# A scan's triangular solve beside the next step's key products, its state kept in PSUM

## The chip, the cores and the metric

The kernel runs on one core of a Trainium2 chip. The metric is the device time of one execution in microseconds (us), the median of three runs. PE is the matmul engine (PEld its weight loads), DVE the vector engine, ACT the scalar engine, POOL the general one, SP the engine that issues the DMAs.

## What is computed

Two layers of a bidirectional encoder run on two groups of 512 tokens, 1024 wide, in 32-bit floats. Layer 0 is RWKV-7 time mixing; its core is a scan per head (16 heads of 64), once forward and once backward in time, and the two results are summed:

```python
def _wkv7_scan(r, decay, k, v, a, b, reverse):
    def step(s, inp):
        r_t, w_t, k_t, v_t, a_t, b_t = inp
        sa = jnp.einsum('bhvk,bhk->bhv', s, a_t)
        s = s * w_t[:, :, None, :] + sa[..., None] * b_t[:, :, None, :] + v_t[..., None] * k_t[:, :, None, :]
        return s, jnp.einsum('bhvk,bhk->bhv', s, r_t)
    ...
    _, y = lax.scan(step, s0, xs, reverse=reverse)
```

Around it stand projections (`xn @ w_r`, `w_k`, `w_v`, `w_z`, an output product with `w_o`), low-rank decays and rates, norms and a SiLU gate. Layer 1 is a neighbourhood attention over an 8 x 64 grid with its own projections. Each layer is normed before and after and added to its input.

## The kernel before

Tokens lie along the free axis, 128 channels (two heads) on the partitions. The scan is done by chunks: 512 tokens are 8 chunks of 64 (`NCH`, `L`). A *pair block* is four heads, `(s, pb)`: group `s` of two, block `pb` of four, so eight of them (`self.todo`), and each takes 8 steps, one chunk of the forward scan and one of the backward scan in each step: 64 steps in all (`self.steps`).

One step (`step`, with `near` and `outer`) does on PE, always with heads on the two halves of the partitions:

- STATE, line 1111: 16 products of the carried state `S` with the chunk's factors, into PSUM tile `zy`; not in a block's first step.
- AKV, line 1117: 8 products with the masked key products `AK`, added to the same tile. ACT scales the sum to `Z` (line 1123).
- SOLVE, line 1133: 8 products of `Z` with the inverse `MT` of the chunk's triangular matrix, into the first half of a bank `us`. ACT copies the two directions into `X` (line 1144); the other half of `X` holds the values, from DMA.
- IDENT, line 1138: in steps 1 to 6 of a block, two products with an identity matrix put the old state into the other half of the bank `us`.
- near, line 1041: 8 key products of the *next* step, into a spare part of `zy`; DVE masks them to `AK` (line 1045).
- SO, line 1149: 8 products over 128 rows add the chunk's own part to the state in `us`; DVE multiplies by the decay and writes the next `S` (line 1159).
- Y, line 1154: 8 products over 128 rows make the outputs; ACT (chunks 0 to 3) or DVE (4 to 7) takes them to `y`.
- OUTER, line 1066: 16 products of 128 columns whose masked results `R` (DVE) and `Tm` (ACT) the step's Y and SO read.

SOLVE and near use 64 x 64 quarters of the array on its diagonal: rows 0 to 63 with columns 0 to 63, and rows 64 to 127 with columns 64 to 127.

While the scan runs, other work fills PE: the *products* (lines 758 to 760, three 128 x 512 matmuls for each of 8 k in a column of weights; 608 such triples) for the projections, `lora` (807, 808) and `grams` (934) for the next block's factors, transposes, and `inverse` (948 on), which inverts the triangular matrices: 30 rounds of two DVE instructions (964, 965), transposes on DVE, then two small sets of products (993, 995). The inverses run one block after another, at a low rank, during the steps of the block before.

The order on PE, DVE and ACT is fixed when the program is built. `weave` takes threads (one each for steps, near, outer, factors, inverse, products and so on) piece by piece; a class `Clock` adds up costs, a piece is taken when its inputs are ready by that clock, and among the ready ones PE pieces come last and the rank decides. A `yield "P"` ends a piece, so that another thread's piece may come between; a change of tile size on PE costs 100 in `Clock.matmul` only where it waits for running tiles.

After the scan the rest (`rest`: the last columns, attention, output products) runs in the scheduler's own order.

Of the kernel before, what the change touches and what calls it, by code (L numbers as in the profile page):

```python
# [18 lines left out]
P = 128  # L19
# [30 lines left out]
class Clock:  # L50
# [132 lines left out]
    def matmul(self, i, ins, n, t):  # L183
# [10 lines left out]
        if self.mode != ts and self.tiles:  # L194
            t = max([t] + [x + 100.0 for x in self.tiles.values()])
            self.tiles = {}
        self.mode = ts
# [36 lines left out]
class Trunk:  # L234
# [782 lines left out]
    def fetch_x(self, st):  # L1017
# [4 lines left out]
        for d in range(2):  # L1022
            self.load(
                st.X[half(1 - e[d]), d].rearrange("t h g c -> t h (g c)"),
                sp["vt", s][pb, i % 2, i // 2, :, :, d].rearrange("h t g c -> t h (g c)"))

    def near(self, q):

        nc, st = self.nc, self.steps[q]
        half = lambda h: slice(64 * h, 64 * h + 64)  # L1030
# [3 lines left out]
            lambda c: max(c.at([st.ab.tensor.name]), 0.0 if q else room(c)))  # L1034
        ab, e = st.ab, st.e
        st.AK = self.t("AK", (P, 2, 2, L), self.NAK, F32, self.front)
        ak = self.steps[q - 1].room if q else self.p("pm", (P, 2, 2, L))
        for g in range(2):
            for dd in range(2):
                for h in range(2):  # L1040
                    nc.tensor.matmul(
                        ak[half(h), dd, g], ab[half(h), dd, g, 1 + e[dd]], ab[half(h), dd, g, 2 - e[dd]], start=not q, stop=True,
                        skip_group_check=True)
        yield "D"
        nc.vector.tensor_tensor(st.AK, ak, self.mstrict.unsqueeze(1).unsqueeze(1).broadcast_to([P, 2, 2, L]), op=ALU.mult)
        self.did["AK"] += 1

    def outer(self, q):
# [9 lines left out]
        for d in range(2):  # L1058
            for g in range(2):
                for a in range(2):  # L1060
                    for h in range(2):
# [5 lines left out]
                            f[half(a), h, 0, d, g] if st.last else f[half(a), h, :, d, g], ab[half(h), d, g, 2 * e[d] + a],  # L1067
# [17 lines left out]
    def step(self, q):  # L1085
# [18 lines left out]
        st.room = zy[:, 0, 256:512].rearrange("p (d g t) -> p d g t", d=2, g=2)  # L1104
# [20 lines left out]
        yield "P", lambda: did["inverse"] > st.n and free2(), lambda c: max(c.at(name(Z, self.formed[key][1])), room2(c))  # L1125
# [3 lines left out]
        for g in range(2):  # L1129
# [703 lines left out]
```

## Time and profile before

| | us |
|---|---|
| median of three runs | 1713.48 (1712.95 to 1714.0) |
| the profiled execution's own time | 1717.21 |
| its span, first to last instruction | 1715.1 |
| PE busy | 1601.5 (93%) |
| DVE busy | 1207.0 (70%) |
| ACT busy | 965.4 (56%) |

The steps run from about 285 to 1067 us of the span. Per-instruction times of small matmuls overlap (each record holds its pipeline's end), so what a bunch of them takes is read from the distance between the starts of one bunch and the next.

### The profile page before, as it was taken

What the parts mean: (1) busy time and instruction counts of PE and PEld (TensorE: products, weight loads), DVE (VectorE), ACT (ScalarE), POOL (GpSimd) and SP (SyncE); (2) the same over time, 40 slices, a digit from 0 to 9 for tenths busy, and PEclk for the clock granted to TensorE, in tenths of its full rate; (3) what the DMA queues carried; (4) which work ended last, traced back from release to release, by engine and by line L of the source; (5) the groups of instructions that cost most, each with busy time, mean ns of one, the idle gap of its engine ahead of it and who ended that gap; (6) DMA issues with size and microseconds to landing.
All of it is one profiled execution on the core that took longest, in us unless ns stands there. A gap on an engine that the chain in (4) does not pass through costs nothing.

```text
span 1715.1 us, 46051 instructions
## 1 busy us (share of the span) xinstructions
PE 1601.5 (93%) x18816; PEld 1229.3 (72%) x18816; DVE 1207.0 (70%) x2645; ACT 965.4 (56%) x1950; POOL 20.7 (1%) x64
## 2 busy tenths in 40 slices
PE   7999879998989999999998878999999999999998
PEld 6766657675756676777776767787777787777776
DVE  8986789695978888898879756423556586555574
ACT  5444766665666485667664533334556665555462
POOL 0000000000000000000000000000000000000000
PEclk9989979898999999999998999999999999999999
DMA  5436778675665677878755756744564247555553
GB/s 205 166 117 208 245 268 262 197 252 188 216 213 187 202 237 228 257 229 252 238 188 175 253 178 201 245 148 153 167 202 135 94 148 270 166 160 166 161 166 99
DMA packets 240820, 336.26 MB, mean 196 GB/s; under 512 B 53696, under 2 KB 119360, under 8 KB 240608
## 3 DMA queue, kind: packets, MB, share of 16 engines
q1 hardware_dynamic: 240608, 333.31, 60.6%
q8 instruction: 148, 2.42, 0.6%
q14 instruction: 64, 0.52, 0.1%
HBM read 227.71 MB, written 105.51 MB: 194 GB/s over the span
## 4 chain that ended last, share of the span: by engine, by line
PE 50%; DVE 8%; ACT 4%; DMA 4%; issue 2%; SPq 0%; DVEq 0%; ACTq 0%
PE pg L424 6%; PE pg L425 5%; PE pg L426 5%; PE pm L758 5%; PE pm L759 4%; PE pm L760 4%; PE pm L1367 3%; PE po L1395 2%; PE pt L1382 2%; PE pf L1066 1%; DMA cab<-dab 1%; PE us L1133 1%; DVE ab L839 1%; PE us L1149 1%; DVE etmp L964 1%
## 5 line engine op out<-in xcount | busy, mean ns | idle before, releaser
L758 PE MATMUL pm<-act,whi 128*128 128x512 f32 x608 | 265.5, 437 | 11.5 <-ACT act L741 7.7
L759 PE MATMUL pm<-act,whi 128*128 128x512 f32 x608 | 245.8, 404 | 8.5 <-DVE act L743 6.9
L760 PE MATMUL pm<-act,wlo 128*128 128x512 f32 x608 | 244.3, 402 | 0.0
L424 PE MATMUL pg<-act,whi 128*128 128x512 f32 x448 | 181.5, 407 | 0.0
L425 PE MATMUL pg<-act,whi 128*128 128x512 f32 x448 | 178.4, 398 | 0.0
L426 PE MATMUL pg<-act,wlo 128*128 128x512 f32 x448 | 177.9, 397 | 0.0
L374 DVE TENSOR_TENSOR wlo<-raw,whi 128x512 fp32r<-128x512 f32 x156 | 107.1, 688 | 91.9 <-ACT whi L373 79.5
L373 ACT CAST whi<-raw 128x512 fp32r<-128x512 f32 x156 | 96.4, 618 | 131.6 <-PE pg L425 62.5
L721 DVE TENSOR_TENSOR wlo<-raw,whi 128x512 fp32r<-128x512 f32 x152 | 103.6, 685 | 82.5 <-ACT whi L719 82.0
L758 PEld LDWEIGHTS pm<-act,whi 128*128 128x128 f32 x608 | 117.7, 194 | 48.8 <-ACT act L741 9.6
L759 PEld LDWEIGHTS pm<-act,whi 128*128 128x128 f32 x608 | 118.2, 194 | 33.3 <-DVE act L743 9.7
L719 ACT CAST whi<-raw 128x512 fp32r<-128x512 f32 x152 | 93.3, 621 | 81.5 <-PE pm L759 69.9
L760 PEld LDWEIGHTS pm<-act,wlo 128*128 128x128 f32 x608 | 118.2, 194 | 26.2
L424 PEld LDWEIGHTS pg<-act,whi 128*128 128x128 f32 x448 | 84.3, 188 | 23.8 <-issue 9.1
L425 PEld LDWEIGHTS pg<-act,whi 128*128 128x128 f32 x448 | 84.3, 188 | 18.4 <-issue 3.5
L426 PEld LDWEIGHTS pg<-act,wlo 128*128 128x128 f32 x448 | 84.2, 188 | 18.2 <-issue 2.2
L965 DVE TENSOR_TENSOR N<-etmp,N 128x30 f32<-128x30 f32 (+14 forms) x240 | 79.8, 332 | 8.3
L1378 ACT ACTIVATE sb<-sb,mx 128x256 f32<-128x256 f32 x128 | 64.1, 502 | 37.7 <-DVE mx L1377 37.2
L1375 DVE CUSTOM_DVE_ANT_0 sb<-pm,bias 128x256 f32<-128x256 f32 x128 | 50.3, 421 | 44.9 <-PE pm L1367 34.1
L964 DVE TENSOR_TENSOR etmp<-N 128x30 f32<-128x30 f32 (+14 forms) x240 | 78.2, 326 | 3.5
L1066 PE MATMUL pf<-cab 64*64 64x128 f32 (+1 forms) x2048 | 69.4, 271 | 8.0 <-DMA cab<-dab 4.5
L1081 ACT COPY Tm<-pf 128x512 f32<-128x512 f32 x56 | 32.8, 587 | 78.0 <-DVE R L1074 78.0
(366 smaller groups left out, 3361.8 us busy)
## 6 DMA issues: line engine op xcount, KB each, us to landing
dab<-ab SPq DMA_DIRECT2D x32, 1024.0 KB
cab<-dab SPq DMA_DIRECT2D x64, 512.0 KB
raw<-in_w_in_dram SPq DMA_DIRECT2D x128, 256.0 KB
bias<-in_rpb_dram SPq DMA_DIRECT2D x32, 384.0 KB
raw<-in_w_z_dram SPq DMA_DIRECT2D x32, 256.0 KB
dz<-tmp SPq DMA_DIRECT2D x32, 256.0 KB
raw<-in_w_k_dram SPq DMA_DIRECT2D x32, 256.0 KB
dk<-tmp SPq DMA_DIRECT2D x32, 256.0 KB
```

Of the source, the lines that this page charges most:

```text
L373: self.nc.scalar.copy(hi, src)
L374: (eng or self.nc.vector).tensor_tensor(lo, src, hi.bitcast(F32), op=ALU.subtract)
L424: nc.tensor.matmul(ps, hi, x[k][0], start=(k == 0), stop=False)
L425: nc.tensor.matmul(ps, hi, x[k][1], start=False, stop=False)
L426: nc.tensor.matmul(ps, lo, x[k][0], start=False, stop=(k == KT - 1))
L719: nc.scalar.copy(hi, raw[h])
L721: nc.vector.tensor_tensor(lo, raw.pop(h), hi.bitcast(F32), op=ALU.subtract)
L758: nc.tensor.matmul(ps, hi[:, at], xh, start=(k == 0), stop=False)
L759: nc.tensor.matmul(ps, hi[:, at], xl, start=False, stop=False)
L760: nc.tensor.matmul(ps, lo[:, at], xh, start=False, stop=(k == KT - 1))
L964: vt.tensor_tensor(tv, N[:, q + 1:, q:q + 1].broadcast_to([P, n, q]), N[:, q:q + 1, :q].broadcast_to([P, n, q]), op=ALU.mult)
L1066: end = nc.tensor.matmul(f[half(a), h, 0, d, g] if st.last else f[half(a), h, :, d, g], ab[half(h), d, g, 2 * e[d] + a], rt if st.last els ...
```

## The change

SOLVE now multiplies half `a` of the rows into half `1 - a` of the columns, the quarters off the diagonal, so `X` keeps its solved part in the other half, its values are loaded into the half that is left, and OUTER writes its rows the other way round. SOLVE's result lies in `zy`, in the spare part that near's results had, and near's results in the same part of the tile's second bank. Where the next chunk's factors are in by the planner's clock when a step's SOLVE is taken, near's 8 products are issued between SOLVE's, two after every other one (`keys_by_step`); else near is a bunch of its own as before.

The bank `us` is now one tile for all steps of a block. SO adds to what stands there, and after DVE has made `S`, ACT copies `S` back into it, in steps 0 to 5 (`act.copy(so, st.S)`); IDENT is gone. There is no `yield` between SO and Y. The planner's clock adds 100 for a change to whole-array matmuls and 50 for other changes of tile size, so that the order changes in many places.

```diff
@@ Clock.matmul
             self.tiles = {}
+            c += 100.0 if ts == (128, 128) else 50.0
@@ fetch_x
-                st.X[half(1 - e[d]), d].rearrange("t h g c -> t h (g c)"),
+                st.X[half(e[d]), d].rearrange("t h g c -> t h (g c)"),
@@ near, its products now in a generator
+    def keys_by_step(self, q, ak):
...
+        for g in range(2):
+            for d in range(2):
+                for h in (1, 0):
+                    nc.tensor.matmul(
+                        ak[half(h), d, g], ab[half(h), d, g, 1 + e[d]], ab[half(h), d, g, 2 - e[d]], start=not q, stop=True,
+                        skip_group_check=True)
+                    yield
@@ outer
-                            f[half(a), h, 0, d, g] if st.last else f[half(a), h, :, d, g], ab[half(h), d, g, 2 * e[d] + a],
+                            f[half(1 - a), h, 0, d, g] if st.last else f[half(1 - a), h, :, d, g], ab[half(h), d, g, 2 * e[d] + a],
@@ step
-        st.room = zy[:, 0, 256:512].rearrange("p (d g t) -> p d g t", d=2, g=2)
+        u = zy[:, 0, 256:512].rearrange("p (h g v) -> p h g v", h=2, g=2)
+        st.room = zy[:, 1, 256:512].rearrange("p (d g t) -> p d g t", d=2, g=2)
...
-        us = self.p("us", (P, 2, 4, HD))
-        u = us[:, 0].rearrange("p (h g) v -> p h g v", h=2)
-        for g in range(2):
-            for h in range(2):
-                for d in range(2):
-                    r = half(e[d])
-                    nc.tensor.matmul(u[r, h, g], mt[r, h, st.i, g], Z[r, h, g], start=True, stop=True)
-        so = us[:, 1].rearrange("p (d g) v -> p d g v", d=2)
-        if st.i and not st.last:
-            for h in range(2):
-                nc.tensor.matmul(
-                    us[half(h), 1].rearrange("p a v -> p (a v)"), self.ident[half(h), 64 * h:64 * h + 64],
-                    before.S[half(h)].rearrange("p d g v -> p (d g v)"), start=True, stop=False, skip_group_check=True)
+        if st.i == 0:
+            self.so = self.p("us", (P, 2, 2, HD))
+        so = self.so
...
+        merged = after and did["fetch"] > q + 1 and self.clock.at([after.ab.tensor.name]) <= self.clock.pe() + self.EPS
+        if merged:
+            k = self.keys_by_step(q + 1, st.room)
+        for g, h in gh:
+            for a in range(2):
+                if a:
+                    next(k, None)
+                    next(k, None)
+                nc.tensor.matmul(
+                    u[half(1 - a), h, g], mt[half(a), h, st.i, g], Z[half(a), h, g], start=False, stop=True, skip_group_check=True)
...
-            yield "P"
...
+        if st.i < NCH - 2:
+            act.copy(so, st.S)
```

By the built programs, 53 of the 64 SOLVE bunches hold the next near; 96 IDENT products are gone and 48 copies have come; PE changes between groups of work with different tile sizes 429 times, where it did 502 times. In the steps of the first six blocks, from the first to the last SOLVE, 101 triples of products stand where 118 did; from the first block's first SOLVE to the last block's last it is 340 for 339. Between a block's first piece of elimination and its seventh `S`, summed over these six, DVE has 238 of 360 elimination instructions where it had 312.

The order on PE in a step, from SOLVE to Y. Before (lines as named above; 758 to 760 are products):

```order
L1133 MATMUL us_8561<-Z_8552,MT_441_1700 64x64 x8
L1138 MATMUL us_8561<-S_8469,cc 64x256 x2
L1041 MATMUL zy_8519<-cab_443_1702 64x64 x8
L758 MATMUL pm_8548<-act_8167,whi_8089 128x512
L759 MATMUL pm_8548<-act_8166,whi_8089 128x512
L760 MATMUL pm_8548<-act_8167,wlo_8090 128x512
L1149 MATMUL us_8561<-X_8311,Tm_8384 64x64 x8
L758 MATMUL pm_8548<-act_8176,whi_8089 128x512
L759 MATMUL pm_8548<-act_8175,whi_8089 128x512
L760 MATMUL pm_8548<-act_8176,wlo_8090 128x512
L1154 MATMUL zy_8519<-X_8311,R_8382 64x64 x8
```

And in the changed kernel, where 1153 is SOLVE, 1038 near, 1076 OUTER, 1167 SO and 1171 Y:

```order
L1153 MATMUL zy_10466<-Z_10500,MT_440_1699 64x64
L1038 MATMUL zy_10466<-cab_442_1701 64x64 x2
L1153 MATMUL zy_10466<-Z_10500,MT_440_1699 64x64 x2
L1038 MATMUL zy_10466<-cab_442_1701 64x64 x2
L1153 MATMUL zy_10466<-Z_10500,MT_440_1699 64x64 x2
L1038 MATMUL zy_10466<-cab_442_1701 64x64 x2
L1153 MATMUL zy_10466<-Z_10500,MT_440_1699 64x64 x2
L1038 MATMUL zy_10466<-cab_442_1701 64x64 x2
L1153 MATMUL zy_10466<-Z_10500,MT_440_1699 64x64
L1076 MATMUL pf_10528<-cab_442_1701 64x2x64 x16
L1167 MATMUL us_9857<-X_10361,Tm_10493 64x64 x8
L1171 MATMUL zy_10466<-X_10361,R_10491 64x64 x8
```

near has moved in between SOLVE's products, IDENT is gone, and Y follows SO with nothing between.

What PE waits for at SO, with the semaphores' engines in brackets (`Activation` is ACT, `DMAHW` a DMA queue). Before:

```order
L1138 MATMUL us_7429<-S_7336,cc 64x256 x2
L1041 MATMUL zy_7371<-cab_442_1701 64x64 x8
L758 MATMUL pm_7416<-act_6262,whi_6719 128x512
L759 MATMUL pm_7416<-act_6261,whi_6719 128x512
L760 MATMUL pm_7416<-act_6262,wlo_6720 128x512
L1149 MATMUL us_7429<-X_7185,Tm_7255 64x64 [waits DMAHW3_49,Activation_49]
L1149 MATMUL us_7429<-X_7185,Tm_7255 64x64 x3
L1149 MATMUL us_7429<-X_7185,Tm_7255 64x64 [waits DMAHW4_49]
L1149 MATMUL us_7429<-X_7185,Tm_7255 64x64 x3
```

In the changed kernel:

```order
L1076 MATMUL pf_8694<-cab_443_1702 64x2x64 x16
L1167 MATMUL us_8144<-X_8503,Tm_8591 64x64 [waits DMAHW3_49,Activation_49]
L1167 MATMUL us_8144<-X_8503,Tm_8591 64x64 x3
L1167 MATMUL us_8144<-X_8503,Tm_8591 64x64 [waits DMAHW4_49,Activation_49]
L1167 MATMUL us_8144<-X_8503,Tm_8591 64x64 x3
L1171 MATMUL zy_8629<-X_8503,R_8585 64x64 [waits DVE_49]
L1171 MATMUL zy_8629<-X_8503,R_8585 64x64 x7
```

SO's two directions now wait for ACT one by one, where the first one waited for both copies that read `us`.

ACT between the outputs of one step and `X` of the next. Before:

```order
L1164 COPY y_6233<-zy_6759 128x256 [waits DVE_49,PE_49]
L863 ACTIVATE e_439_1696<-thw_6486 128x8x64 [waits DVE_49,Activation_49]
L866 ACTIVATE e_1322_6927<-thw_6486 128x512
L1123 ACTIVATE Z_6948<-zy_6899 128x256 [waits PE_49]
L869 ACTIVATE pp_6950<-tha_6509,dv 128x512
L872 COPY wc_6671<-e_439_1696 128x8 [waits Activation_49]
L1081 COPY Tm_6968<-pf_6931 128x512 [waits DVE_49]
L1144 COPY X_6754<-us_6955 64x256 [waits PE_49]
```

In the changed kernel (1181 is the copy of the outputs, 1185 the new copy, 1091 `Tm`, 1134 `Z`, 1162 `X`):

```order
L1181 COPY y_6034<-zy_6035 128x256 [waits DVE_49,PE_49]
L1185 COPY us_6639<-S_6685 128x256 [waits DVE_49]
L1091 COPY Tm_6753<-pf_6700 128x512 [waits DVE_49]
L1134 ACTIVATE Z_6761<-zy_6726 128x256 [waits PE_49]
L1162 COPY X_6018<-zy_6726 64x256 [waits PE_49]
```

The new copy stands behind the copy of the outputs, waits for DVE's `S`, and has `Tm` and `Z` queued behind it.

## Rows read from the trace of the kernel before

**Rows 1.** Busy us by engine: stretch, length, PE to POOL, clock, DMA share.
```profile
285.00:1080.00 795.00, 724.85 (x14077) 553.04 (x14076) 629.41 (x1216) 476.79 (x947) 15.15 (x16) 0.96 0.69 216
...
1080.00:1715.00 635.00, 625.33 (x3264) 486.36 (x3262) 344.67 (x1006) 327.55 (x707) 0.00 (x0) 1.00 0.51 166
```

**Rows 2.** The same of one dense stretch, and the sum over six of them.
```profile
728.00:779.00 51.00, 49.77 (x1138) 37.96 (x1133) 47.11 (x102) 32.06 (x72) 0.00 (x0) 1.00 0.75 233
...
sum 333.00, PE 315.24 PEld 238.27 DVE 287.55 ACT 206.93 POOL 0.00; mean PE 52.54 PEld 39.71 DVE 47.92 ACT 34.49 POOL 0.00
```

**Rows 3.** The same of the last two pairs of heads.
```profile
961.00:1066.00 105.00, 85.60 (x2255) 69.94 (x2251) 64.27 (x113) 40.75 (x92) 0.00 (x0) 0.97 0.63 199
```

**Rows 4.** Timeline of PE in one step, with the state of DVE: start us, us, instruction.
```profile
727.34 0.68 PE L1133 MATMUL us<-Z,MT 64*64 64x64 f32 x16
727.85 0.63 PE L1041 MATMUL zy<-cab 64*64 64x64 f32 x16
728.41 0.50 PE L758 MATMUL pm<-act,whi 128*128 128x512 f32 x1
728.75 0.39 PE L759 MATMUL pm<-act,whi 128*128 128x512 f32 x1
728.98 0.40 PE L760 MATMUL pm<-act,wlo 128*128 128x512 f32 x1
729.43 0.69 PE L1149 MATMUL us<-X,Tm 128*64 128x64 f32 x16
730.05 0.50 PE L758 MATMUL pm<-act,whi 128*128 128x512 f32 x1
...
730.61 0.40 PE L760 MATMUL pm<-act,wlo 128*128 128x512 f32 x1
730.94 0.69 PE L1154 MATMUL zy<-X,R 128*64 128x64 f32 x16
...
731.64 0.42 DVE L1159 TENSOR_TENSOR S<-us,wc 128x256 f32<-128x256 f32 x1
...
733.06 0.64 PE L1111 MATMUL zy<-S,cab 64*64 64x64 f32 x32
733.53 0.41 PE L1117 MATMUL zy<-V,AK 64*64 64x64 f32 x16
```

**Rows 5.** Timeline of PE in the next step.
```profile
735.41 0.68 PE L1133 MATMUL us<-Z,MT 64*64 64x64 f32 x16 [0.58 <-ACT Z L1123]
735.93 0.60 PE L1138 MATMUL us<-S,cc 64*64 64x256 f32 x4
736.36 0.63 PE L1041 MATMUL zy<-cab 64*64 64x64 f32 x16
```

**Rows 6.** Timeline of a step near the end: from X to the outputs.
```profile
986.05 0.74 ACT L1144 COPY X<-us 64x256 f32<-64x256 f32 x2 [1.22 <-PE us L1138]
...
986.85 0.69 PE L1149 MATMUL us<-X,Tm 128*64 128x64 f32 x16 [0.39 <-ACT X L1144]
...
987.37 0.64 PE L1154 MATMUL zy<-X,R 128*64 128x64 f32 x16
```

**Rows 7.** Waits from 285 to 1080: who waited for whom, us in total, times, longest.
```profile
ACT Tm L1081 <- DVE R L1074: 78.0, 53, 4.0
ACT Z L1123 <- PE zy L1117: 50.1, 34, 3.7
...
PE us L1149 <- ACT X L1144: 7.5, 11, 1.8
```

**Rows 8.** Groups by line: count, busy us, mean ns, idle time before them.
```profile
L1081 ACT COPY Tm<-pf 128x512 f32<-128x512 f32 x56 | 32.8, 587 | 78.0 <-DVE R L1074 78.0
...
L1123 ACT ACTIVATE Z<-zy 128x256 f32<-128x256 f32 x64 | 24.6, 385 | 50.4 <-PE zy L1117 50.1
...
L1282 ACT ACTIVATE tmp<-tmp 128x512 f32<-128x512 f32 x8 | 5.0, 629 | 0.0
...
L965 DVE TENSOR_TENSOR N<-etmp,N 128x168 f32<-128x168 f32 (+14 forms) x217 | 71.7, 330 | 7.5
```

More of the change, by code (lines that the diff above doesn't have):

```diff
@@ L1033, in near @@
             "P", lambda: self.did["fetch"] > q and (self.did["solve"] >= q if q else free()),
[L1034 to L1037, printed above, removed]
-        for g in range(2):
-            for dd in range(2):
-                for h in range(2):
-                    nc.tensor.matmul(
[L1042 to L1045, printed above, removed]
+            lambda c: 0.0 if st.ak is not None else max(c.at([st.ab.tensor.name]), 0.0 if q else room(c)))
+        if st.ak is None:
+            run(self.keys_by_step(q, self.steps[q - 1].room if q else self.p("pm", (P, 2, 2, L))))
+            yield "D"
+        else:
+            yield "D", None, lambda c: st.done
+        nc.vector.tensor_tensor(st.AK, st.ak, self.mstrict.unsqueeze(1).unsqueeze(1).broadcast_to([P, 2, 2, L]), op=ALU.mult)
         self.did["AK"] += 1
@@ L1124, in step @@
         free2, room2 = self.bank("us")
-        yield "P", lambda: did["inverse"] > st.n and free2(), lambda c: max(c.at(name(Z, self.formed[key][1])), room2(c))
+        yield (
+            "P", lambda: did["inverse"] > st.n and (st.i > 0 or free2()),
+            lambda c: max(c.at(name(Z, self.formed[key][1])), 0.0 if st.i else room2(c)))
         mt = self.formed[key][1].rearrange("p (h i g) a t -> p h i g (a t)", h=2, i=NCH)
-        us = self.p("us", (P, 2, 4, HD))
-        u = us[:, 0].rearrange("p (h g) v -> p h g v", h=2)
-        for g in range(2):
-            for h in range(2):
-                for d in range(2):
-                    r = half(e[d])
-                    nc.tensor.matmul(u[r, h, g], mt[r, h, st.i, g], Z[r, h, g], start=True, stop=True)
-        so = us[:, 1].rearrange("p (d g) v -> p d g v", d=2)
-        if st.i and not st.last:
-            for h in range(2):
+        if st.i == 0:
+            self.so = self.p("us", (P, 2, 2, HD))
+        so = self.so
+        k = iter(())
+        after = self.steps[q + 1] if q + 1 < len(self.steps) else None
+        merged = after and did["fetch"] > q + 1 and self.clock.at([after.ab.tensor.name]) <= self.clock.pe() + self.EPS
[6 more added lines that the diff above has]
+                    next(k, None)
                 nc.tensor.matmul(
-                    us[half(h), 1].rearrange("p a v -> p (a v)"), self.ident[half(h), 64 * h:64 * h + 64],
-                    before.S[half(h)].rearrange("p d g v -> p (d g v)"), start=True, stop=False, skip_group_check=True)
+                    u[half(1 - a), h, g], mt[half(a), h, st.i, g], Z[half(a), h, g], start=False, stop=True, skip_group_check=True)
+        run(k)
+        if merged:
+            after.done = self.clock.note()
         did["solve"] += 1
@@ L1143, in step @@
         for d in range(2):
-            act.copy(st.X[half(e[d]), d], u[half(e[d])])
+            r = half(1 - e[d])
+            act.copy(st.X[r, d], u[r])
         yield "P", lambda: did["R"] > q and did["X"] > q, lambda c: c.at(name(st.X, st.R[0], *([] if st.last else st.Tm[:1])))
@@ L1148, in step @@
                 for g, h in gh:
-                    nc.tensor.matmul(so[half(h), d, g], st.Tm[d][:, h, g], st.X[:, d, h, g], start=(st.i == 0), stop=True, skip_group_check=True)
-            yield "P"
+                    nc.tensor.matmul(so[half(h), d, g], st.Tm[d][:, h, g], st.X[:, d, h, g], start=st.i == d == g == 0, stop=True, skip_group_check=True)
         for g, h in gh:
@@ L1155, in step @@
         if not st.last:
-            yield "D", None, lambda c: c.at(name(us))
+            yield "D", None, lambda c: c.at(name(so))
             st.S = t("S", (P, 2, 2, HD), 2)
@@ L1717, in __init__ @@
         self.last = i == NCH - 1
+        self.ak = None
 def both(*gs):
```

6 lines of the change are left out of this document (5 added, 1 removed).

## Prediction

> **What bounds the kernel now.** I read the busy time by stretches first. From 285 to 1080 us, where the scan runs, PE is busy for 724.85 of 795 us and DVE for 629.41, 79% [rows 1]. After 1080 PE is busy for 625.33 of 635 us [rows 1]: there is no slack behind the scan, and products that don't fit into it are simply done later. So what the scan costs is PE's own work plus the 70 us in which PE stands idle. Two reservations. In the stretches where a block's steps run close together DVE is nearly full too: six of them add up to 333 us with DVE busy for 287.55, 86%, and the fullest has 47.11 of 51, 92% [rows 2]. And in the last two blocks the products have run out; PE is busy for 85.60 of 105 us and the chain of each step decides [rows 3]. The second view is PE's timeline of single steps, read by distances between starts [rows 4 to 6]; the third is what ACT and PE wait for [rows 7, 8].
>
> A price in a profiled execution stands against that execution's own time, 1717.2 us, which is 3.7 us above the median of the three runs; I take the 3.7 off at the end.
>
> **SOLVE beside near.** In a step without IDENT, SOLVE starts at 727.34, near at 727.85 and the next product at 728.41 [rows 4]: 1.07 us for the two. Eight products on diagonal quarters take 0.51, while STATE, with sixteen of the same size on all four quarters, takes 0.47 (733.06 to 733.53) [rows 4]. So two quarters that share output columns and differ in rows run together, two on the diagonal don't. The merged bunch is issued in such pairs, SOLVE from rows 0 to 63 and near from 64 to 127 into the same columns, then the other way round, and the two write different banks as STATE's do. It should take STATE's 0.47, and with the change to a product behind it (0.10, as after near and SO) 0.57. That is 0.50 less, in 53 steps: **26.5 us**. The Trainium skill says otherwise ("TensorEngine Tiling (Array Packing)", Key Properties: different tiles execute loads and matmuls in parallel). By that, SOLVE's two diagonal quarters had already overlapped, eight on two of them would take half of the 0.51, and the merged bunch half of the 0.47, some 12 us less in sum than the 26.5 already counts; the 0.51 speaks against it, and I stay with pairs.
>
> **IDENT.** From its start to near's is 0.43 (735.93 to 736.36) [rows 5]; 48 steps give **20.6 us** of PE.
>
> **One bunch for SO and Y, and fewer changes.** From SO to a product is 0.62 (729.43 to 730.05), from SO straight to Y 0.52 (986.85 to 987.37); the first product after small ones takes 0.34 to the next, a following one 0.23, and the last one before Y 0.33 [rows 4, 6]. One excursion to products and back thus costs 0.10 + 0.11 + 0.10 = 0.31, or 0.155 for a change. The order has 73 changes fewer: **11.3 us**. Products that stood between SO and Y are not gone; they stand elsewhere.
>
> That makes 58.4 us of PE's work. Against it:
>
> **The chain in the last blocks.** There PE's work is not what counts. `X` waited for IDENT, since both used the bank `us` (start 986.05) [rows 6]; without it each of 12 steps starts 0.43 earlier. SO waited for both copies of `X`, 0.74, and starts 0.06 after them [rows 6]; now its first half can go after one copy, and as the second half still needs the other, what is won is the half bunch, 0.26, in 14 steps. That is 5.2 + 3.6 = 8.8, where a quarter of 58.4 would be 14.6: **6 us** of the gain are lost.
>
> **The copies on ACT.** No row shows ACT writing PSUM. The nearest: `Z`, 128 x 256 from PSUM, takes 0.385; a 128 x 512 copy takes 0.587 from PSUM and 0.629 from the other memory [rows 8]. So 0.43 each, 20.5 us in all, on an engine that is busy for 476.79 of 795 us [rows 1]. (The Trainium skill, "ScalarE: Activation LUTs", Step-by-step: what each stage is for, has ACT write faster to PSUM; no run here shows that yet, and the copies would then be somewhat below this.) The copy is needed by the next step's SO, a whole step later, so nobody waits for it itself. What stands behind it is `Z`. In 34 of 64 steps ACT idles 1.5 us on average before `Z`, for PE [rows 7], and there it costs nothing; in the other 30 it can push `Z` back: 30/64 x 48 x 0.43 = 9.7 us at most. PE has other bunches to issue meanwhile in about half of the cases: **5 us**, with ends 0 and 20.5. The new wait for `S` adds little at `Z`, because PE's STATE, which `Z` needs, waits for `S` as well.
>
> **DVE in the dense stretches.** Six of eight blocks, 48 steps, lose 58.4 x 48/64 = 43.8 us of PE's work, and the 17 triples that moved out take 17 x 3 x 0.23 = 11.7 along: 333 would become 277.5. DVE's work there falls by the 74 elimination instructions that moved behind the steps, at 0.33 [rows 8]: 287.55 - 24.4 = 263.1. That would be 95%, more than any of these stretches shows. At the 92% of the fullest they need 284.7: **7 us** back. At today's 86% they would need 304.7, 27 us back. I take the first, since the fullest stretch is the one whose PE had most work, too, and products fill what is left.
>
> Loads by SP are the same in number and size; `X`'s go to other partitions. SO's waits for `X` on PE, 7.5 us now [rows 7], lose near and IDENT as cover between SOLVE and SO, but `X` itself may start 0.43 earlier and SO's first half goes after one copy: I put it at nothing, with 7.5 us to win or to lose.
>
> **Sum.** 1717.2 - 58.4 + 6 + 5 + 7 = 1676.8, less 3.7: **1673 us**, 2.4% faster.
>
> **Rivals.**
> 1. *DVE sets the dense stretches*, at the share it has now: 27 us instead of 7 come back: 1693. For it: the inverses run one after another, and the order has moved 74 of their instructions behind the steps, where a block then waits for them. Against it: 92% occurs already.
> 2. *The quarters don't run together* when SOLVE and near mix, the change does not do what it says: 26.5 us are lost, 1699. Against it stands STATE's 0.47.
> 3. *ACT stands at the new copy, slower than before.* In the step of rows 4, `S` ended at 732.06, 2.63 after SO's start, because DVE had other work first. Y straight behind SO ends 1.16 after SO's start [rows 6], and the copy of the outputs 0.39 later: the new copy then waits 1.08 and takes 0.43, 1.5 us in which casts, `Tm` and `Z` stand behind it. `Tm` waits for DVE's `R` in just this way, 78 us in 53 times [rows 7]. If all 48 land on PE, 72 us take the place of the 5: 1740. It makes the kernel slower once some 45 of the 72 us reach PE, 0.94 us per copy. Against it: ACT is idle or waiting for 40% of the scan.
> 4. *The waits shrink, too.* With the chain of a step shorter by 0.69 us the wait for `X` vanishes, and none of the three losses shows but the last blocks': 1717.2 - 58.4 + 6 - 7.5 - 3.7 = 1654, down to 1648 without that one.
>
> **How the numbers follow.** The forecast has a chance of 0.52, DVE 0.16, the quarters 0.06, ACT 0.13 (of which 0.04 lies within the bound of no change), shrinking waits 0.13. The range from 1650 to 1702 holds the first three and most of the last; what is left out is ACT's case and the end of the last, some 0.17. A measurement of this kernel can tell 0.2%, 3.4 us, from no change. Faster 0.87, same 0.04, slower 0.09.
>
> **What would show it.** The distance from a merged bunch's first start to the next product: 0.57 if right, 1.0 if the quarters don't pair. PE's busy time in the scan some 55 us lower, with its idle time no more than 20 us above the 70. A group of 48 copies into `us` at about 0.43, with idle time before them for DVE's `S`: over 45 us would be rival 3. DVE's share in the dense stretches: near 92%, or near 86% with those stretches over 300 us in sum, rival 1. The forecast is wrong if PE's idle time grows by 40 us or more, or if the gaps between blocks grow by what the steps save.

## The result: slower by 1.5%

The changed kernel takes 1738.02 us (median of 4 runs, 1730.08 to 1741.77), the kernel before in the same session 1713.22 (1703.74 to 1714.0): a ratio of 1.0147, 95% interval 1.0107 to 1.0187. The forecast was 1673, with a range to 1702. The profiled execution of the changed kernel took 1735.46 us, 18.25 more than that of before. Unless said otherwise, times of one execution are compared with that execution of before (span 1715.1), and medians with the median of before in the same session. Executions of the kernel before lie between 1704 and 1724 us over all sessions, so a few us between two profiled executions say little by themselves.

The page of the changed kernel, its span and its first part (busy us, share, instructions):

```profile
span 1733.7 us, 45757 instructions
...
PE 1573.1 (91%) x18624; PEld 1201.5 (69%) x18624; DVE 1206.3 (70%) x2645; ACT 979.8 (57%) x2000; POOL 20.7 (1%) x64
```

PE is busy 28.4 us less than the 1601.5 of before, and the span is 18.6 us longer: PE stands idle for 160.6 us instead of 113.6. The windows that answer to [rows 1]:

```profile
285.00:1080.00 795.00, 688.70 (x13927) 520.53 (x13928) 625.98 (x1212) 492.06 (x1001) 15.18 (x16) 0.95 0.70 216
1080.00:1733.00 653.00, 640.80 (x3316) 498.16 (x3314) 350.16 (x1014) 332.79 (x716) 0.00 (x0) 0.99 0.51 164
```

In the scan PE works 36 us less than before, and the scan still ends at about the same time; behind it the kernel needs 18 us more. A cut at a fixed time hides how the two hang together. The cut that tells is the end of the last Y, the last product of the last step. It starts here (timeline of PE, first before, then after):

```profile
1068.45 0.69 PE L1154 MATMUL zy<-X,R 128*64 128x64 f32 x16
```

```profile
1062.24 0.69 PE L1171 MATMUL zy<-X,R 128*64 128x64 f32 x16 [0.84 <-ACT X L1162]
```

Windows of before up to the end of the last Y and behind it (stretch, length, PE, PEld, DVE, ACT, POOL, clock, DMA):

```profile
285.00:1069.10 784.10, 713.95 (x14030) 544.34 (x14028) 619.94 (x1202) 472.94 (x940) 15.15 (x16) 0.96 0.69 218
1069.10:1715.10 646.00, 636.23 (x3312) 495.06 (x3310) 354.14 (x1019) 331.40 (x714) 0.00 (x0) 1.00 0.51 165
```

The same of the changed kernel:

```profile
285.00:1062.90 777.90, 678.10 (x13906) 515.58 (x13906) 612.12 (x1192) 487.52 (x993) 15.18 (x16) 0.95 0.70 218
1062.90:1733.70 670.80, 651.41 (x3339) 503.10 (x3337) 364.02 (x1035) 337.34 (x724) 0.00 (x0) 0.98 0.51 163
```

That is the account of the whole change, in these two executions: **6.2 us won up to the last Y, 24.8 us lost behind it**, 18.6 in sum. The loss behind the last Y is firm: eleven runs below that keep the order of before have 645 to 649 us there, the changed kernel and the two runs with its picks 670.8 to 672.5. The 6.2 is not: the medians differ by 24.8 in all, the same figure by chance, which leaves nothing won before the last Y. Of the 35.9 us that PE works less in the scan, 29.6 have become idle time (70.2 before, 99.8 after). Behind the last Y there are 27 more matmuls (3339 against 3312), nine triples of products; PE is busy 15.2 us longer, and idle 19.4 instead of 9.8.

The local prices came out nearly as forecast. The timeline of PE of the changed kernel, from SO to the bunch that merges SOLVE (L1153) and near (L1038):

```profile
736.65 0.73 PE L1167 MATMUL us<-X,Tm 128*64 128x64 f32 x16
737.39 0.69 PE L1171 MATMUL zy<-X,R 128*64 128x64 f32 x16
738.00 0.50 PE L759 MATMUL pm<-act,whi 128*128 128x512 f32 x1
...
740.68 0.22 PE L1153 MATMUL zy<-Z,MT 64*64 64x64 f32 x2
...
741.25 0.66 PE L680 MATMUL pm<-cc,tmp 128*128 128x128 f32 x4
```

The merged bunch takes 0.57 here (740.68 to 741.25), the number forecast; over the 29 merged bunches that a 128 x 512 matmul follows, the median is 0.60. The new copy, and the old one of `X`, as groups of ACT:

```profile
L1162 ACT COPY X<-zy 64x256 f32<-64x256 f32 x128 | 47.0, 367 | 54.2 <-PE zy L1153 45.4 <-PE zy L1038 4.9 <-DMA X<-dvt 2.2
...
L1185 ACT COPY us<-S 128x256 f32<-128x256 f32 x48 | 18.3, 381 | 6.8 <-DVE S L1176 6.8
```

381 ns a copy, and 6.8 us of waiting for `S` in all: ACT does not stand there. What is new stands elsewhere. Waits of DVE from 285 to 1080 (who waited for whom, us in total, times, longest):

```profile
DVE AK L1055 <- ACT X L1162: 39.2, 41, 3.2
```

and of PE, in the same stretch:

```profile
PE pm L759 <- ACT act L742: 10.4, 7, 3.4
PE pm L760 <- DVE act L744: 9.7, 11, 2.2
PE zy L1122 <- ACT y L1181: 7.2, 7, 1.8
...
PE zy L1153 <- ACT Z L1134: 5.9, 12, 0.8
...
PE us L1167 <- ACT X L1162: 2.8, 6, 0.6
```

Before, AK waited for `X` 3.3 us and for near 21.2 (group of DVE):

```profile
L1045 DVE TENSOR_TENSOR AK<-zy,cc 128x256 f32<-128x256 f32 x63 | 26.6, 422 | 24.7 <-PE zy L1041 21.2 <-ACT X L1144 3.3
```

And the chain of waits from 285 to 1080, by line, before and after (the view itself ends where these lines do):

```profile
by line: PE pm L758 6.9%; PE pm L759 5.7%; PE pm L760 5.5%; issue 4.3%; PE pf L1066 3.0%; DMA cab<-dab 2.8%; PE us L1133 2.1%; DVE ab L839 1.9%; PE us L1149 1.8%; DVE etmp L964 1.8%; DVE R L1074 1.7%; DVE N L965 1.7%; PE zy L1154 1.7%; ACT 
```

```profile
by line: DMA cab<-dab 8.6%; issue 6.2%; PE pm L759 5.9%; PE pm L760 4.9%; PE pm L761 4.6%; PE pf L1076 4.2%; PE zy L1122 2.4%; PE us L1167 2.1%; PE zy L1153 2.0%; ACT X L1162 1.8%; PE pm L996 1.6%; PE zy L1038 1.6%; PE zy L1171 1.6%; PE pm 
```

So four suspects: the order that the planner now makes, AK's wait for `X`, the loads of the factors (`cab`), and the pace of the scan itself, which did not follow PE's saving.

### The profile page after: what moved, and what is told of

The parts are those of the page before. It is cut to its first block, busy times and chain, and to the rows that moved or that the text cites. A ratio compares the mean times of both kernels' runs of the same rounds, so it can differ in the third digit from the quotient of the medians.

```text
span 1733.7 us, 45757 instructions
## 1 busy us (share of the span) xinstructions
PE 1573.1 (91%) x18624; PEld 1201.5 (69%) x18624; DVE 1206.3 (70%) x2645; ACT 979.8 (57%) x2000; POOL 20.7 (1%) x64
## 4 chain that ended last, share of the span: by engine, by line
PE 52%; DVE 8%; ACT 7%; DMA 7%; issue 3%; SPq 0%; DVEq 0%; ACTq 0%
PE pg L425 6%; PE pg L426 6%; PE pg L427 5%; PE pm L759 5%; PE pm L760 4%; PE pm L761 4%; DMA cab<-dab 4%; PE pm L1386 3%; PE pf L1076 2%; PE po L1414 2%; PE pt L1401 2%; PE zy L1122 1%; PE us L1167 1%; PE zy L1153 1%; ACT X L1162 1%
## 5 line engine op out<-in xcount | busy, mean ns | idle before, releaser
L759 PE MATMUL pm<-act,whi 128*128 128x512 f32 x608 | 267.3, 440 | 27.4 <-ACT act L742 20.2
L760 PE MATMUL pm<-act,whi 128*128 128x512 f32 x608 | 249.4, 410 | 17.6 <-DVE act L744 15.9
L1076 PE MATMUL pf<-cab 64*64 64x128 f32 (+1 forms) x2048 | 74.1, 276 | 15.0 <-DMA cab<-dab 5.9
L1162 ACT COPY X<-zy 64x256 f32<-64x256 f32 x128 | 47.0, 367 | 54.2 <-PE zy L1153 45.4
```

The costliest lines, as they stand in the source:

```text
L759: nc.tensor.matmul(ps, hi[:, at], xh, start=(k == 0), stop=False)
L760: nc.tensor.matmul(ps, hi[:, at], xl, start=False, stop=False)
L1076: end = nc.tensor.matmul(f[half(1 - a), h, 0, d, g] if st.last else f[half(1 - a), h, :, d, g], ab[half(h), d, g, 2 * e[d] + a], rt if st. ...
```

## Experiments: the order or the operations

The planner's model is deterministic, so an order can be written down as the list of its picks and followed with other operations. Two theories. O: the operations save what was forecast, and the new order loses it. W: the operations bring waits of their own.

**x_ops**: the changed operations, the picks of before.

```diff
     def weave(self, threads):
...
-        ck = self.clock
-        while True:
...
+        for c in ORDER:
+            t = threads[ord(c) - 65]
             t.step()
...
-        merged = after and did["fetch"] > q + 1 and self.clock.at([after.ab.tensor.name]) <= self.clock.pe() + self.EPS
+        merged = after and did["fetch"] > q + 1
...
                     nc.tensor.matmul(so[half(h), d, g], st.Tm[d][:, h, g], st.X[:, d, h, g], start=st.i == d == g == 0, stop=True, skip_group_check=True)
+            yield "P"
```

> The changed operations in the order of before: every piece is taken where the kernel before takes it, and SO and Y stay apart; near is issued between SOLVE's products, IDENT is gone, ACT copies the state back. Theory O (the planner's new order is what costs, the operations themselves save PE's time as forecast): 47 us less of PE's work (26.5 + 20.6), of which some 12 go to the waits, so about 1678 (1660 to 1695). Theory W (the operations bring waits of their own, the key mask on DVE behind X above all, that eat the gain in any order): 1715 to 1740, with DVE idle for 35 us or more before the key mask.

Measured: 1716.51 against 1715.22, ratio 1.0006 (0.9985 to 1.0028). The changed operations are worth nothing in the order of before, though 62 bunches are merged in it. That is the time that theory W gave; the 1678 of theory O is out. Its windows:

```profile
285.00:1065.60 780.60, 678.15 (x13807) 510.69 (x13799) 616.75 (x1197) 485.67 (x985) 15.13 (x16) 0.95 0.70 218
1065.60:1711.50 645.90, 635.71 (x3310) 494.77 (x3310) 354.04 (x1019) 331.04 (x714) 0.00 (x0) 1.00 0.51 165
```

The part behind the last Y is that of before to 0.1 us; PE's 35.8 us in the scan have become 32.3 us of idle time. Where PE stands, from 285 to 1080:

```profile
PE us L1203 <- ACT X L1198: 19.8, 22, 3.1
PE zy L1189 <- ACT Z L1170: 9.8, 17, 1.6
PE zy L1208 <- DVE AK L1091: 8.3, 8, 2.1
PE pf L971 <- ACT Tm L1127: 7.2, 6, 2.0
```

These are the links of a step: SO for `X` (7.5 before, [rows 7]), SOLVE for `Z`, Y for AK, the Gram matrices for `Tm`. And one step in it, by ACT, PE and DVE:

```profile
735.60 0.76 ACT L1198 COPY X<-zy 64x256 f32<-64x256 f32 x2 [0.29 <-PE zy L1189]
...
736.38 0.69 PE L1203 MATMUL us<-X,Tm 128*64 128x64 f32 x16
736.38 0.42 DVE L1091 TENSOR_TENSOR AK<-zy,cc 128x256 f32<-128x256 f32 x1 [0.94 <-ACT X L1198]
```

The keys are ready with the merged bunch, but AK begins only when both copies of `X` are through, and DVE idles 0.94 us for it: keys and solution now lie in the two banks of one tile. Whether the shared tile is what keeps AK back, x_us tests below.

**y_order**: the converse, the operations of before and the picks of the changed kernel, with Y at once behind SO.

```diff
-            yield "P"
+            yield "P", "at once"
...
+        for c in ORDER:
+            t = threads[ord(c) - 65]
             t.step()
...
+            if t.gate == "at once":
+                t.step()
...
```

> The operations of before in the order of the changed kernel: SOLVE and near apart on diagonal quarters, IDENT kept, S not copied back; every piece is taken where the changed kernel takes it, Y at once behind SO. Theory O: the order alone costs, so slower than the changed kernel, 1760 to 1790. Theory W: the order is harmless, and without the new waits this is 1700 to 1720, DVE idle before the key mask for about 25 us as before.

Measured: 1748.51, ratio 1.0195 (1.0157 to 1.0233). Its part behind the last Y:

```profile
1070.60:1741.50 670.90, 652.63 (x3337) 503.57 (x3337) 363.94 (x1035) 336.94 (x724) 0.00 (x0) 0.98 0.51 163
```

670.9, as in the changed kernel (670.8), and 24.9 more than before; up to the last Y it needs only 1.5 more than before. The cost of this order lies behind the scan, with the old operations as with the new. Neither theory had the time: it lies under O's range and over W's. And in this order the changed operations do seem to gain a little: y_order stands 33.3 us over before, the changed kernel 24.8, some 8 us less, though the two intervals (1.0157 to 1.0233 and 1.0107 to 1.0187) overlap.

**e_clock** and **e_noclock**: the new planner cost alone, and the change without it.

```diff
             self.tiles = {}
+            c += 100.0 if ts == (128, 128) else 50.0
```

> The kernel before with the planner's new cost for a change of tile size alone; no operation changes. Theory O, if that cost is what spoils the order: 1735 to 1780. If the order is spoilt by the shorter steps and not by this cost, or by theory W: 1700 to 1720.

> The changed kernel without the planner's new cost for a change of tile size. Theory O with this cost as the culprit: 1665 to 1695. Theory O with another part as the culprit: 1725 to 1745. Theory W: 1725 to 1745, since all the new waits are still there.

Measured: 1749.05, ratio 1.0201 (1.0160 to 1.0242), and 1738.02, ratio 1.0133 (1.0083 to 1.0182). The cost alone spoils the old order by 34 us; without it the changed operations get yet another order, which is as slow as theirs with it. But e_clock's order does not lose its time where the changed kernel's does. Its windows up to the end of the last Y and behind it:

```profile
285.00:1107.00 822.00, 724.42 (x14117) 547.27 (x14116) 623.74 (x1204) 480.40 (x952) 15.13 (x16) 0.96 0.67 208
1107.00:1755.30 648.30, 638.40 (x3320) 496.82 (x3319) 355.62 (x1022) 332.41 (x717) 0.00 (x0) 1.00 0.52 166
```

The last Y ends 37.9 us later than before, and the part behind it needs 2.3 more: this order is slow within the scan. An order can lose on either side of the last Y.

**e_jit** and **a_jit**: next to no change of the planner, in the kernel before and in the changed one.

```diff
-        c += 66.0
+        c += 67.0
```

> The kernel before with one number of its planner's model changed by next to nothing: 67 ns in place of 66 ns of fixed cost for an instruction of DVE. Operations are unchanged; the order changes in about as many places as with the cost of a tile change (2450 lines of PE's order against 2930). Theory T (the order of before is a picked one, and any other of this planner costs as much): 1732 to 1752. Theory C (the cost of a tile change itself plans badly): 1708 to 1720.

> The changed kernel with 67 in place of 66 ns of fixed cost for an instruction of DVE in its planner: another order of the same operations, different in 3266 lines of PE's. If orders of this planner differ by chance, it lies anywhere from 1715 to 1760, and more than 5 us away from 1738. If the changed operations themselves set the time, it stands within 5 us of 1738.

Measured: 1726.89, ratio 1.0072 (1.0049 to 1.0096), and 1730.31, ratio 1.0083 (1.0051 to 1.0115). (a_jit does not compute the kernel's second output; why stayed open, and only its time is used.) One nanosecond in the model costs 13 us in the kernel before, and takes 9 off the changed one (24.8 over before, now 15.8). Neither theory of e_jit had its range right: an order made anew is slower, but not always by 20 us.

How many product triples an order leaves behind the last Y can be counted in the order itself, and goes along with the time of that part in the profiled executions (end of the last Y, and time behind it, us; e_rank follows below):

| kernel | triples behind | to the last Y | behind |
|---|---|---|---|
| before, x_ops | 150 | 1069.1, 1065.6 | 646.0, 645.9 |
| e_clock | 153 | 1107.0 | 648.3 |
| e_jit | 155 | 1061.4 | 657.0 |
| e_noclock | 156 | 1072.8 | 660.4 |
| a_jit | 157 | 1056.2 | 668.2 |
| e_rank | 158 | 1141.8 | 670.8 |
| after, y_order | 159 | 1062.9, 1070.6 | 670.8, 670.9 |

The time behind grows with the triples without an exception, and from 155 on by more than these cost; the time up to the last Y does not follow them. Nine triples are 27 x 0.23 = 6.2 us ([rows 4]: 0.23 from product to product). Of the other 18.6 of the 24.8, 9.6 are idle time and 9.0 are matmuls taking longer. The products right behind the last Y find their operands not cast yet. Groups of PE behind the last Y, before and then after (mean ns, idle time before them):

```profile
L758 PE MATMUL pm<-act,whi 128*128 128x512 f32 x150 | 59.5, 397 | 0.0
```

```profile
L759 PE MATMUL pm<-act,whi 128*128 128x512 f32 x159 | 64.4, 405 | 7.8 <-ACT act L742 7.6
```

and the stretch in question, 1063 to 1120, before and after:

```profile
1063.00:1120.00 57.00, 55.63 (x327) 44.45 (x326) 26.02 (x38) 22.68 (x38) 0.00 (x0) 1.00 0.64 219
```

```profile
1063.00:1120.00 57.00, 47.20 (x166) 33.33 (x167) 27.48 (x41) 18.77 (x31) 0.00 (x0) 0.85 0.60 194
```

PE idles for 9.8 of these 57 us, where it idled for 1.4 before, and the granted clock is 0.85, a mix of its two levels of 1.2 and 2.4 GHz, where it was 1.00. This is read from the trace; no run moved these casts.

**e_rank**: an attempt at a better order of the changed kernel, with the inverse's rank ahead of the next block's factors.

```diff
...
-Thread(lambda: 5, inverse())
+Thread(lambda: 1.3, inverse())
...
```

> The changed kernel with one number of its planner changed: the rank of the inverse 1.3 in place of 5, so that DVE takes the elimination ahead of the factors and the weights' halves. Theory I: the inverses end earlier, blocks start up to 10 us sooner each, 1700 to 1728. Otherwise (DVE's work only changes places, or the order is worse for it): 1733 to 1760.

Measured: 1811.61, ratio 1.0565 (1.0524 to 1.0605). Both ranges are missed. The first four eliminations end earlier than in the changed kernel (the first at 273 us, not at 295), the other four later (the fifth at 740, not at 710), and the last Y ends at 1141.8, 78.9 later; 670.8 us follow, as in the changed kernel. This order, too, loses its time within the scan.

## Experiments: what sets the pace of the scan

All of these but a_nocab follow the order of before, so that only the operations differ, and the part behind the last Y stays between 645 and 649 us in every one of them. The expectations name further theories: P, that time saved on PE is time of the kernel; B, that the scan runs at the pace of its blocks, and PE's saving becomes idle time.

**x_carry** and **x_merge**: each half of the change alone. x_carry is x_ops with SOLVE and near apart; x_merge is x_ops with IDENT in place of the copy.

```diff
-        merged = after and did["fetch"] > q + 1
+        merged = None
```

```diff
-        if st.i < NCH - 2:
-            act.copy(so, st.S)
...
+                nc.tensor.matmul(
+                    so[half(h)].rearrange("p d g v -> p (d g v)"), self.ident[half(h), 64 * h:64 * h + 64],
...
```

> The order of the kernel before; of the changed operations only the carry in PSUM (copy of S into the bank, no IDENT) and the quarters that it uses; SOLVE and the next keys stay two bunches. PE loses 20.6 us of IDENT, and ACT gains 48 copies of 0.38 us. Theory W: AK still stands behind X, but near follows later here, so that it costs little: 1698 to 1708. Theory B: 1706 to 1716, as with IDENT left out and nothing put in its place.

> The order of the kernel before; of the changed operations only SOLVE beside the next keys, with IDENT and its carry kept as before. PE loses about 53 x 0.50 = 26 us and no copy is added. Theory W: AK is ready 0.5 us earlier and stands behind X for it, so that the saving is eaten and the time is 1712 to 1722. Theory P (PE's time is the kernel's): 1689 (1684 to 1696). Theory B: 1704 to 1716.

Measured against 1713.41: 1715.41, ratio 1.0018 (0.9998 to 1.0039), and 1716.19, ratio 1.0016 (0.9989 to 1.0043). Neither half gains. DVE idles before AK for `X` in both, 38.0 and 41.1 us: in x_carry, too, where near is a bunch of its own, and theory W had it cheap there. x_carry lies in theory B's range, x_merge in W's; P is out.

**x_noident** and **x_us**: IDENT left out and nothing put in its place; and the changed operations, with the solution `u` in the bank of the next state instead of `zy`, so that AK and `X` read different tiles. In both the next state loses its carry, so neither computes the kernel's outputs.

```diff
-                nc.tensor.matmul(
-                    us[half(h), 1].rearrange("p a v -> p (a v)"), self.ident[half(h), 64 * h:64 * h + 64],
...
```

```diff
+            self.so = self.p("us", (P, 2, 4, HD))
+        so = self.so[:, 1].rearrange("p (d g) v -> p d g v", d=2)
+        u = self.so[:, 0].rearrange("p (h g) v -> p h g v", h=2)
...
```

> The kernel before, in its own order of pieces, with one thing left out: the identity products that carry the state (IDENT), so that each state loses its carry. Nothing is added and no wait is new. IDENT took 48 x 0.43 = 20.6 us of PE. Theory P (in the scan, time that PE saves is time of the kernel): 1715 - 20 = 1695 (1690 to 1700). Theory B (the scan runs at the pace of its blocks, which DVE, the inverses and the loads set; PE's saving turns into idle time): less than half of it, 1705 to 1715, with PE idle up by 10 us or more.

> The changed operations in the order of the kernel before, and the solution u in the free half of the bank of the next state, so that AK and X no longer read one tile and AK need not stand behind X (the start flag of u clears the bank, so that the next state loses its carry; instructions are the same in number and kind). Theory W (AK's wait for X, 42 us of idle DVE, is what ate the saving): that idle time falls below 10 us and the time goes to 1680 to 1698. Theory B (pace of the blocks): the idle time of DVE only changes its name, 1706 to 1717.

Measured: 1707.89, ratio 0.9977 (0.9951 to 1.0004), and 1707.12, ratio 0.9975 (0.9948 to 1.0003): 5.5 and 6.3 us, at the edge of what can be told from nothing. AK as a group of DVE in x_ops, and then in x_us:

```profile
L1091 DVE TENSOR_TENSOR AK<-zy,cc 128x256 f32<-128x256 f32 x63 | 26.6, 423 | 42.4 <-ACT X L1198 41.9
```

```profile
L1091 DVE TENSOR_TENSOR AK<-zy,cc 128x256 f32<-128x256 f32 x63 | 26.3, 418 | 9.2 <-PE us L1189 8.9 <-PE zy L1074 0.3
```

So the wait for `X` is real and comes from the shared tile, and taking it away is worth some 7.6 us (x_ops stands 1.3 over the kernel before, x_us 6.3 under it, each known to about 4), not the 20 or more that theory W put on it. Both runs lie in theory B's ranges. Most of what is given back is found at one other link. PE's longest wait in x_noident, and in x_us:

```profile
PE us L1180 <- ACT X L1175: 17.2, 20, 3.3
```

```profile
PE us L1203 <- ACT X L1198: 27.3, 31, 3.2
```

SO waits for `X`, as in [rows 7], 7.5 us there. IDENT and near were what PE did while ACT copied [rows 5]; with less of it PE waits for the same copies.

**x_elim** and **x_both**: three of the 30 steps of each elimination left out, alone and together with IDENT.

```diff
+            if q in (14, 15, 16):
+                continue
```

> The kernel before in its own order, with three of the 30 steps of each elimination (14, 15 and 16: a product and a sum on DVE each) left out, so that the inverses are not the inverses. That is about 48 instructions of 0.4 us, 19 us of DVE. Theory I (the blocks follow one another at the pace of the inverses: an elimination starts when the inverse before it is done, and DVE is 85 to 98% busy in it): of the 2.4 us per inverse six or seven come through, 1696 to 1703. Theory P (PE sets the time): 1711 to 1716. Theory J (DVE and PE wait for each other in one fixed order, so that either alone gives a quarter to a third of what it saves): 1705 to 1710.

> The kernel before in its own order, with the identity products (20.6 us of PE) and the three elimination steps (19 us of DVE) left out together. Theory I: hardly more than the elimination steps alone, 1692 to 1700. Theory J: the two together give clearly more than the sum of each alone, 20 us or more: 1680 to 1695.

Measured against 1713.42: 1713.53, ratio 0.9996 (0.9971 to 1.0022), and 1709.64, ratio 0.9980 (0.9960 to 1.0000). Nineteen us less on DVE, within the chain of the inverses, are worth nothing, and with IDENT gone as well the two are worth no more than IDENT alone. Theories I (the inverses set the pace) and J (PE and DVE wait for each other) are out; theory P had x_elim right, but x_noident had already ruled it out.

**a_nocab, b_nocab, x_nocab**: the loads of the factors left out from the third step on, in the changed kernel, in the one before, and in x_ops.

```diff
-        self.load(cab[:, :16 * L], sp["ab", s, pb][i].rearrange("p d g a -> p (d g a)"))
+        if self.steps.index(st) < 2:
+            self.load(cab[:, :16 * L], sp["ab", s, pb][i].rearrange("p d g a -> p (d g a)"))
```

> The changed kernel in its own order, with the loads of the factors into the two buffers cab left out from the third step on (all later steps use the data of the first two): nothing waits for these loads and for the buffers. Theory K (in the changed order these loads take the path: 8.5% of the chain between 285 and 1085 us, some 68 us, against 2.8%, 22 us, before): 1738 falls by 30 us or more, to 1690 to 1708. Theory R (the order's cost is spread over waits of all engines): 1718 to 1732.

> The kernel before in its own order, with the same loads left out. Both theories: little to gain, 1698 to 1712. Theory K: the distance to the changed kernel without these loads falls from 25 us to under 8. Theory R: it stays at 15 us or more.

> The changed operations in the order of the kernel before, with the same loads left out. If the loads are what keeps the steps from using the time that PE saves, this is faster than before without its loads by 15 us or more (1680 to 1695). If the pace is set by the engines' fixed order, it stands within 8 us of it (1695 to 1712).

Measured against 1714.49: 1720.11, ratio 1.0028 (1.0002 to 1.0054); 1699.58, ratio 0.9922 (0.9898 to 0.9946); 1700.61, ratio 0.9927 (0.9907 to 0.9948). The loads cost 15 to 19 us in every order: 19 in the changed kernel (24.8 over before, now 5.6), where the chain names them at 8.6%, and 15 in the kernel before, where it names them at 2.8%. They are not what the new order loses, as theory R had it: without them the distance between the two kernels is still 20.5 us. And with them gone the changed operations still gain nothing (1.0 us between b_nocab and x_nocab).

**b_pool** and **x_pool**: the same loads issued by GpSimd instead of SyncE, in before and in x_ops.

```diff
-        self.load(cab[:, :16 * L], sp["ab", s, pb][i].rearrange("p d g a -> p (d g a)"))
+        self.nc.gpsimd.dma_start(cab[:, :16 * L], sp["ab", s, pb][i].rearrange("p d g a -> p (d g a)"))
```

> The changed operations in the order of the kernel before, with the loads of the factors (cab) issued by GpSimd in place of SyncE, whose queue waits most of the time (SPq behind Y alone 68 us in the kernel before) with these loads behind it. Theory Q (the place in SP's queue is what the loads' 15 us come from): 1700 to 1710, faster than both kernels. Theory T (the two buffers and the transfer itself are): 1712 to 1722. If GpSimd issues more slowly than SyncE: over 1722.

> The kernel before in its own order with the same loads issued by GpSimd. Theory Q: 1699 to 1709. Theory T: 1711 to 1718. If the changed operations can use loads that come earlier, x_pool is faster than this by more than 5 us; if not, the two are within 5 us.

Measured against 1715.88: 1722.83, ratio 1.0041 (1.0015 to 1.0066), and 1714.39, ratio 0.9977 (0.9954 to 1.0001). The queue was not it, theory Q is out. Theory T has b_pool right; x_pool lies just over its range and 8.4 us over b_pool, and why is open. A third buffer for `cab` was not tried. No kernel that computes the whole result was clearly faster than before.

## Why the prediction was wrong, step by step

- **The prices on PE were right.** The merged bunch takes 0.60 in the median, 0.57 forecast, and the quarters pair; rival 2 is out. Y follows SO after 0.51 in the median of 56 steps, as in [rows 6] (0.74 in the one shown, 736.65 to 737.39). The new copies take 0.381 each, 0.43 forecast (48 of these are 20.6 us, not 20.5). The Trainium skill ("ScalarE: Activation LUTs", Step-by-step: what each stage is for) has ACT write faster to PSUM; the 0.381 lies below my estimate, but the trace does not bear the rule out: the copy of the outputs, of the same size and from PSUM to SBUF, takes 0.369 (L1181, 32 copies), and no copy here differs from another in its destination alone. One count was off: the order merges 48 bunches; in five more near follows SOLVE as a bunch of its own, with nothing between, and I had counted these as merged (2.5 us).
- **The step that failed first is the one from work to time**: "what the scan costs is PE's own work plus the 70 us in which PE stands idle", with the 70 held fixed. PE's work in the scan did fall, by 35.9 us; its idle time rose from 70.2 to 99.8. In the old order (x_ops) it works 35.8 less and idles 32.3 more, and of the 47 us that SOLVE beside near and IDENT were to give, none came. IDENT shows it in its pure form: 20.6 us of instructions, and leaving them out gives 5.5. I had read the three steps of [rows 4 to 6] by distances between starts on PE, and had not asked what PE would do in the freed time, with the order fixed and the next bunch waiting for a copy on ACT.
- **"SO's waits for X ... I put it at nothing"**, with 7.5 us to win or lose. They went to 19.8 in x_ops and 27.3 in x_us. In the changed kernel they are 2.8, since its order puts other bunches there; the idle time is then before the products (`act`, 20.1 us) and STATE.
- **AK behind X was not in the list.** It cost 39.2 us of DVE's time; in the order of before the wait was worth some 7.6 of the kernel's.
- **The order was taken as a gain of 11.3 us** for 73 fewer changes of tile. It lost 24.8 behind the last Y. The 17 triples that left the dense stretches are not those behind the scan: they stand between the blocks or in the last two, since the scan holds 340 triples where it held 339. The nine more behind the last Y are eight that stood before the first SOLVE (109 are left there of 117) and two from between the last SOLVE and the last Y, less the one more in the scan. I had not counted them, and this could be counted before any run. That their operands would be late, and the clock lower, could not.
- **DVE (7 us, rival 1)** did not set the dense stretches. From a block's first SOLVE to the end of its seventh Y, summed over the six blocks, before and after:

```profile
sum 330.86, PE 313.38 PEld 237.63 DVE 284.12 ACT 209.05 POOL 0.00; mean PE 52.23 PEld 39.60 DVE 47.35 ACT 34.84 POOL 0.00
```

```profile
sum 281.82, PE 250.60 PEld 193.61 DVE 229.21 ACT 181.96 POOL 0.00; mean PE 41.77 PEld 32.27 DVE 38.20 ACT 30.33 POOL 0.00
```

The stretches shrank from 330.9 us (333 by the cut of [rows 2]) to 281.8, about as the 284.7 forecast, with DVE at 229.2, 81%, and not 92%. But what lies between these stretches, up to the next block's first SOLVE, grew from 310.4 to 352.5 us: 42.1 of the 49.1 that the steps saved. Most of this is the order's doing: y_order has 287.1 and 357.8 with the old operations, x_ops 326.5 and 311.4 with the new ones. In the old order 19 us less of DVE changed nothing; in the new one no run took work from DVE.
- **Rival 3, the slower one, had the right time for the wrong reason**: 1740, by ACT standing at the copy. It stood there 6.8 us.
- **The signs of failure were named rightly**: PE's idle time grew by 47 us over the kernel (29.6 up to the last Y), and the gaps between blocks grew by most of what the steps saved.

What stays open: which link sets the pace of the scan in the order of before. It is not PE's work, nor DVE's, nor both at 20 us each; the loads of the factors account for 15 us; the waits of a step for ACT's copies took much of what PE saved, but no run made these copies shorter. Open, too, is why e_clock's and e_rank's orders are slow within the scan.

## What to carry over

In a kernel whose engines follow one fixed order, a saving on the busiest engine is worth what the next link leaves of it: name what the engine waits for once the work is gone, since here that work was cover for another engine's copy. If a planner makes the order, count first what it leaves behind the last dependent step (it can lose before it as well), and test the change in the old order, replayed, before judging it: here one nanosecond in the planner's model moved the kernel by 13 us, and the whole change in the old order by 1. And a line's share of the chain of waits is no price: 8.6% and 2.8% of it came to 19 and 15 us.

## Unexpected

- The products behind the scan take longer after a stretch with idle time: the granted clock is 0.85 from 1063 to 1120 us, where PE idled for 9.8 us, and 1.00 before. Of the 24.8 us behind the last Y only 6.2 are further matmuls.
- Loads issued by GpSimd gained nothing, though SyncE's queue stood behind Y alone for 68.2 us of the scan in the kernel before: 1714.39 against 1715.88 there, and 6 us slower than x_ops (1722.83, against 1716.51 in another session) with the changed operations. In the profiled executions PE's waits for `cab` fell from 6.2 to 1.5 us (before and b_pool), so the loads were late less often, and the time of the kernel did not follow.
- An SBUF to PSUM copy of 128 x 256 on ACT takes 381 ns, about what the scaled copy `Z` out of PSUM takes (385, [rows 8]) and the plain one of the outputs (369).
